# Queries and keys of an attention layer by full Strassen products, in a rewritten fixed order of four engines

## The chip, the cores and the metric

The kernel runs on one core of a Trainium2 chip. The metric is the time of one execution on the device in microseconds (us); the kernel before was run three times, and their median is 1639.4 us. A core has five engines with instruction queues of their own, each worked off in order: PE (matmuls and transposes), DVE and ACT (element-wise work, both also on the accumulators in PSUM), POOL (element-wise work in on-chip memory only) and SP, which here issues the DMAs.

## The reference

A decoder trunk of two layers on one sequence of 1024 tokens with 1024 features, in float32. Layer 0 is attention in three dilated groups, layer 1 a diagonal state-space layer. The change concerns layer 0:

```python
def dilated_attention_mixer(h, w_in, w_out, rel_bias):
    proj = h @ w_in                          # (1024 x 1024) @ (1024 x 10240)
    qkv = proj[..., :n_qkv].reshape(B, S, 3, N_GROUPS_A, ATTN_HEADS, HEAD_DIM)
    z = proj[..., n_qkv:]
    for g, (window, dilation) in enumerate(DILATED_GROUPS):   # (128,1) (512,4) (2048,16)
        o, l = dilated_group_attention(qkv[:, :, 0, g], qkv[:, :, 1, g], qkv[:, :, 2, g], ...)
        ...
    wts = jax.nn.softmax(jnp.stack(lses), axis=0)             # the groups are merged
    o = jnp.sum(wts[..., None] * jnp.stack(outs), axis=0)
    return (o * jax.nn.silu(z)) @ w_out
```

`h` is the normalised input. Before and after the mixer stand an RMS norm each, and the result is added to the input.

## The kernel before

**Precision.** Every operand of a large matmul is split into a high part (rounded to the fast float32 format `F32R`) and a low part (what the rounding left): `split` casts on ACT (L104) and subtracts on another engine (L105). A product then takes three matmuls: high x high, low x high, high x low.

**Strassen.** The normalised rows stand transposed on chip as `c.h[th]`: th is a half of the tokens (512), and each holds eight k-tiles of 128 features, as high and low parts. Taken as 2 x 2 blocks (th, kh), with kh a half of the features, they make a product of 2 x 2 blocks possible with seven block products instead of eight (Winograd's form). The class `Quads` adds up the row sums that this needs, `self.rows = [a11, a12, s4, a22, s1, s2, s3]`; a block has four k-tiles. The values of the attention are made this way early (L440) and go to DRAM (`v_dr`).

**Units.** Queries and keys are made in the attention stage by 24 units, one for a pair of heads p and a group g each. A unit's two raw weight tiles (512 KB each, pool `wraw` with two buffers) are the columns of q and of k: these are the two column halves of the Strassen form. Between the two stages the memory holds only two of four k-tiles of each row sum: the tile of a sum is a `Halves` object of two pieces, one in the pool `pf`, which stays, and one in the pool `vphase`, which is closed. So a unit does seven Strassen products (`form`) on k-tiles 0, 1 of each half, and k-tiles 2, 3 by plain products (`straight`). `product(n)`, n from 0 to 9, accumulates all of this in two PSUM banks, X and Y; `sums(n)` copies or adds what is to be kept, and `qk(n)` splits the results into the tiles q and k that the logits read. All these matmuls have the line L567.

**Order.** The function `attn_units` runs 26 steps. In step m, unit m (`cur`) does its products, unit m-1 (`one`) its logits and exponentials and the first of its weighted sums of values (PV), and unit m-2 (`two`) the rest of them, while the weights of unit m+1 (`nxt`) are loaded and split. The object `Program` pins the order in which the instructions are written for each of PE, ACT, DVE and POOL; SP's order is left to the scheduler. So a helper's instruction that must wait holds up whatever is written behind it on the same engine. On PE the order of a step is

```
product 0, 1 | PV T | logits 0 | product 2, 3 | PV T | logits 1 | product 4, 5 | PV ptm |
logits 2 | product 6, 7 | logits 3 | T | product 8, 9 | PV T
```

where T are the transposes of exponentials (L726), PV is L775, logits are L698 with their bias and maximum on DVE (L704), ptm is the transpose of the statistics in `put_ms` (L802). POOL makes the low parts of the weights (L105) and their differences (L541), the low parts of q and k, the rotations for layer 1 and the merge of the groups (L953, L954). Buffers that the change touches: the bias tile `T` (two), the split exponentials `ph` (three), `vp` for all eight blocks of a unit's values, `wsp` with four weight tiles, and `w5`, `w6` of their own.

**Gates.** After the units, `attn_gate` multiplies both token halves with the columns of z for four pairs of heads (the other four are done early), so it needs all of `c.h` again.

Of the kernel before, what the change touches and what calls it, by code (L numbers as in the profile page):

```python
# [56 lines left out]
class Halves:  # L57


    def __init__(self, *parts):  # L60
        self.parts = parts

    def __getitem__(self, at):
        p, k, cols = at if len(at) == 3 else at + (slice(None),)
        if isinstance(k, slice):
            return self.parts[k.start // 2][p, :, cols]
        return self.parts[k // 2][p, k % 2, cols]
# [181 lines left out]
def load_bias(c, p, g):  # L249


    t = c.attn.tile([P, 2, 256], F32, tag="T", name="T", bufs=2)
    at = 0 if g < 2 else P
    src = bass.AP(c.vec_dr.tensor, c.vec_dr.offset + (g * 16 + 2 * p) * 384 + at, [[1, P], [384, 2], [1, 256 - at]])
    c.nc.sync.dma_start(t[:, :, at:256], src)
    return t


def evac_q(c, ps, g, t0, q):

    n = ps.shape[1] // ORD[g]
    at = (S - t0) // ORD[g] - n
    hi, lo = (t.rearrange("p (r l) -> p r l", r=ORD[g])[:, :, at:at + n] for t in q)
    split(c, hi, lo, ps.rearrange("p (l r) -> p r l", r=ORD[g])[:, :, ::-1], 0.125)

# [43 lines left out]
class Quads:  # L309
# [4 lines left out]
    def __init__(self, c):  # L314
# [3 lines left out]
        def part(th, kh):  # L318
            return [t[:, 4 * kh:4 * kh + 4, :] for t in c.h[th]]
# [3 lines left out]
        def tt(o, x, y, op):  # L323
            for n in (slice(0, 2), slice(2, 4)):
                nc.vector.tensor_tensor(o[:, n], x[:, n], y[:, n], op=op)

        def parts(slots, t):
            hi, lo = (c.vslot(s, F32R) for s in slots)
            for n in (slice(0, 2), slice(2, 4)):
                split(c, hi[:, n], lo[:, n], t[:, n])  # L330
            return hi, lo
# [19 lines left out]
        self.rows = c.forms = [a11, a12, s4, a22, s1, s2, s3]  # L351
        t2, t3 = c.vslot(2, F32), c.vslot(3, F32)
        self.sums = [t2[:, 0:2], t2[:, 2:4], t3[:, 0:2]]
        self.tmp = t3[:, 2:4].rearrange("p a x -> p (a x)")

# [150 lines left out]
class Unit:  # L506
# [6 lines left out]
    def __init__(self, c, m):  # L513
        self.c = c
        self.p, self.g = divmod(m, 3)
        self.engine = c.nc.gpsimd if m else c.nc.vector
        self.p1 = self.u2 = self.u3 = None
        self.lg, self.pt, self.ph, self.po = {}, {}, {}, {}
# [3 lines left out]
    def load(self, w_in):  # L522
        c = self.c
        with c.tc.high_priority(AHEAD):
            self.raw = []
            for n in range(2):
                t = c.wraw.tile([P, KT * P], F32, tag="wraw", name="wraw")
                c.nc.sync.dma_start(t, w_in[(3 * n + self.g) * 8 + self.p])
                self.raw.append(t.rearrange("p (a b x) -> p a b x", a=2, b=2))

    def halves(self, src, tag, pool=None):
        c = self.c
        w = (pool or c.wsp).tile([P, 2] + list(src.shape[1:]), F32R, tag=tag, name=tag, bufs=1 if pool else 4)
        c.last_lo = split(c, w[:, 0], w[:, 1], src, engine=self.engine).ins
        return w

    def weights(self, n):
        c = self.c
        q, k = self.raw
        def sub(o, x, y):  # L540
            self.engine.tensor_tensor(o, x, y, op=ALU.subtract)  # L541

        b11, b21, b12, b22 = q[:, 0, 0], q[:, 1, 0], k[:, 0, 0], k[:, 1, 0]
        if n == 0:
            self.w1 = self.halves(q[:, :, 0], "w")
            sub(b11, b12, b11)
            sub(b12, b22, b12)
        elif n == 1:
            self.w6 = self.halves(b22.unsqueeze(1), "w6", c.attn)
            sub(b22, b22, b11)  # L550
            sub(b21, b21, b22)
        elif n == 2:
            self.w2 = self.halves(q[:, :, 1], "w")
        elif n == 3:
            self.w3 = self.halves(k[:, :, 0], "w")
        elif n == 4:
            self.w4 = self.halves(q[:, :, 0], "w")
        else:
            self.w5 = self.halves(k[:, :, 1], "w5", c.attn)
# [3 lines left out]
    def block(self, ps, w, a, rows, ks, start, stop):  # L563
        c = self.c
        order = [(b, x, y) for b in range(2) for x, y in ((0, 0), (1, 0), (0, 1))]
        for m, (b, x, y) in enumerate(order):
            c.nc.tensor.matmul(ps, w[:, y, a, b * P:b * P + P], rows[x][:, ks + b, :], start=start and m == 0,  # L567
                                      stop=stop and m == 5, skip_group_check=True)

    def form(self, ps, i, w, a, start=False, stop=True):  # L570
        self.block(ps, w, a, self.c.forms[i], 0, start, stop)

    def straight(self, ps, w, th, start=False, stop=True):
        self.block(ps, w, 0, self.c.h[th], 2, start, False)
        self.block(ps, w, 1, self.c.h[th], 6, False, stop)

    def order(self, ps, reverse):

        t = ps.rearrange("p (l r) -> p r l", r=ORD[self.g])
        return t[:, :, ::-1] if reverse else t  # L580

    def copy(self, name):
        t = self.c.slot(name, tag="a").rearrange("p (r l) -> p r l", r=ORD[self.g])
        if name == "p1":
            self.c.nc.scalar.activation(t, self.order(self.X, True), AF.Copy, scale=0.125)
        else:
            self.c.nc.scalar.copy(t, self.order(self.X, False))
        return t

    def add(self, t):  # L590
        v, y = self.c.nc.vector, self.order(self.Y, t is self.p1)
        if t is self.p1:
            v.scalar_tensor_tensor(t, y, 0.125, t, op0=ALU.mult, op1=ALU.add)
        else:
            v.tensor_tensor(t, t, y, op=ALU.add)  # L595

    def bank(self, n):
        c = self.c
        return (c.psx, c.psy)[n].tile([P, H], F32, tag="xy"[n], name="xy"[n])

    def product(self, n):
        if n == 0:
            self.X = self.bank(0)
            self.form(self.X, 0, self.w1, 0, start=True)
        elif n == 1:
            self.Y = self.bank(1)
            self.straight(self.Y, self.w2, 0, start=True, stop=False)
        elif n == 2:
            self.form(self.X, 5, self.w3, 1)
        elif n == 3:  # L610
            self.form(self.Y, 1, self.w1, 1)
        elif n == 4:
            self.form(self.X, 6, self.w3, 0)
        elif n == 5:
            self.Y = self.bank(1)
            self.form(self.Y, 2, self.w6, 0, start=True, stop=False)
            self.straight(self.Y, self.w5, 0)
        elif n == 6:
            self.straight(self.X, self.w2, 1, stop=False)
        elif n == 7:  # L620
            self.Y = self.bank(1)
            self.form(self.Y, 4, self.w4, 0, start=True)
        elif n == 8:
            self.form(self.X, 3, self.w4, 1)
        else:
            self.straight(self.Y, self.w5, 1)

    def sums(self, n):
        if n == 0:
            self.p1 = self.copy("p1")  # L630
        elif n == 2:
            self.u2 = self.copy("u2")
        elif n == 4:
            self.u3 = self.copy("u3")
        else:
            self.add(getattr(self, {3: "p1", 5: "u2", 7: "u2", 9: "u3"}[n]))

    def qk(self, n):
        c, g = self.c, self.g
        if n == 0:  # L640
            self.q, self.k = ([c.attn.tile([P, S], F32R, tag=x + y, name=x + y, bufs=1) for y in "hl"] for x in "qk")
        if n == 1:
            evac_q(c, self.X, g, H, self.q)
            return
        src = (self.p1, None, self.u2, self.u3)[n]
        w = H // ORD[g]
        at = 0 if n == 2 else w
        hi, lo = (t.rearrange("p (r l) -> p r l", r=ORD[g])[:, :, at:at + w] for t in (self.k if n else self.q))
        split(c, hi, lo, src, engine=c.nc.gpsimd)
# [3 lines left out]
    def load_v(self):  # L653
        c, p, g = self.c, self.p, self.g
        self.vp = vp = c.attn.tile([P, KT, P], F32, tag="vp", name="vp", bufs=1)
        o = ORD[g]
        off = c.v_dr.offset + (g * 2 + p // 4) * S * H + p % 4 * P
        for dst, at, step in (((vp, 0, P),), ((vp[:, 0::2], 0, 1), (vp[:, 1::2], o * P, 1)), ((vp, 0, 1),))[g]:
            src = bass.AP(c.v_dr.tensor, off + at * H, [[o * H, P], [step * H, dst.shape[1]], [1, P]])
            c.nc.sync.dma_start(dst, src)  # L660
        self.bt = load_bias(c, p, g)

    def split_v(self):
        c, vp = self.c, self.vp
        self.v = vs = c.attn.tile([P, KT, 2, P], F32R, tag="vs", name="vs", bufs=1)
# [63 lines left out]
    def split_weights(self, u, x):  # L729
        c = self.c  # L730
        parts = []
        for pt, wd in self.pt.pop((u, x)):
            t = c.attn.tile([P, 2, H], F32R, tag="ph", name="ph", bufs=3)
# [148 lines left out]
def attn_units(c, w_in):  # L882
# [7 lines left out]
    for n in (0, 2, 1, 3, 4, 5):  # L890
        units[0].weights(n)
    for m in range(26):
# [13 lines left out]
        if m:  # L906
            run((cur, "weights", 5))
        if one and one.g == 0:
            step(rotations, c, one.p, 0)
            step(rotations, c, one.p, 1)  # L910
        if two and c.merge is not None:
            if two.g == 0:
                step(merge_weights, c, c.merge)
            step(merge, c, c.merge, c.outputs[c.merge], two.g)
# [1089 lines left out]
```

## Time and profile before

| | |
|---|---|
| three runs | 1637.63, 1639.40, 1639.65 us |
| profiled execution | 1634.66 us, its span 1632.8 us |
| granted TensorE clock | 0.996 |
| busy share PE / DVE / ACT / POOL | 98 / 65 / 47 / 42% |
| attention stage (first to last matmul of L567) | about 339 to 1062 us |

The lines of the profile name line, engine and operation, what is written and what is read, the shapes, the count, then the busy time of the group in us, the mean of one instruction in ns, and the idle time of the engine before them with what ended it. Timeline rows give start and duration in us. Rows of stretches give, for each engine, busy us and number of instructions, then the TensorE clock, the DMA engines' share and GB/s. The matmul durations overlap, as matmuls are pipelined; their starts tell the pace.

### The profile page before, as it was taken

What the parts mean: (1) busy time and instruction counts of PE and PEld (TensorE: products, weight loads), DVE (VectorE), ACT (ScalarE), POOL (GpSimd) and SP (SyncE); (2) the same over time, 40 slices, a digit from 0 to 9 for tenths busy, and PEclk for the clock granted to TensorE, in tenths of its full rate; (3) what the DMA queues carried; (4) which work ended last, traced back from release to release, by engine and by line L of the source; (5) the groups of instructions that cost most, each with busy time, mean ns of one, the idle gap of its engine ahead of it and who ended that gap; (6) DMA issues with size and microseconds to landing.
All of it is one profiled execution on the core that took longest, in us unless ns stands there. A gap on an engine that the chain in (4) does not pass through costs nothing.

```text
span 1632.8 us, 26979 instructions
## 1 busy us (share of the span) xinstructions
PE 1606.7 (98%) x9606; PEld 1368.8 (84%) x9606; DVE 1060.0 (65%) x2563; ACT 773.9 (47%) x1904; POOL 689.7 (42%) x579
## 2 busy tenths in 40 slices
PE   8999999999999999999999999999999999989998
PEld 6889999988888888888888888887888888878886
DVE  8799899835565565655565565748563899855533
ACT  5232233236656666666666666655353233334411
POOL 1000000055557767675768767533220455422121
PEclk9999999999999999999999999999999999999999
DMA  6123445442232332333233332327346988665532
GB/s 253 65 53 110 157 146 162 138 148 58 77 95 82 98 111 72 101 95 96 80 92 111 86 124 79 122 66 196 128 152 184 262 247 241 198 194 161 174 101 86
DMA packets 184720, 212.24 MB, mean 130 GB/s; under 512 B 42484, under 2 KB 138503, under 8 KB 184585
## 3 DMA queue, kind: packets, MB, share of 16 engines
q1 hardware_dynamic: 184584, 210.52, 43.0%
q8 instruction: 75, 1.23, 0.3%
q14 instruction: 61, 0.49, 0.1%
HBM read 153.51 MB, written 56.96 MB: 129 GB/s over the span
## 4 chain that ended last, share of the span: by engine, by line
PE 88%; DVE 6%; DMA 4%; issue 1%; POOL 1%; ACT 1%; SPq 0%; DVEq 0%; ACTq 0%; POOLq 0%
PE y L567 18%; PE psj L130 16%; PE x L567 13%; PE psq L440 10%; PE pso L1180 10%; PE pso L775 5%; PE psl L698 5%; PE pt L726 4%; PE psv L298 2%; PE psb L130 1%; DMA v<-in_x_dram 1%; DVE T L1706 1%; PE pst L147 1%; DVE T L1711 1%; PE pv L1699 1%
## 5 line engine op out<-in xcount | busy, mean ns | idle before, releaser
L567 PE MATMUL y<-hh,w 128*128 128x512 f32 x672 | 225.5, 393 | 0.0
L105 POOL TENSOR_TENSOR w<-wraw,w 128x512 fp32r<-128x512 f32 x138 | 164.5, 1199 | 135.0 <-ACT w L104 130.3
L720 ACT ACTIVATE lg<-lg,nm 128x128 f32<-128x128 f32 (+1 forms) x384 | 168.5, 442 | 36.7 <-DVE nm L715 36.5
L567 PEld LDWEIGHTS y<-hh,w 128*128 128x128 f32 x672 | 126.3, 188 | 28.9
L567 PE MATMUL x<-hh,w 128*128 128x512 f32 x384 | 138.0, 410 | 0.0
L567 PE MATMUL y<-hl,w 128*128 128x512 f32 x336 | 131.6, 392 | 0.0
L1558 POOL TENSOR_TENSOR Ks<-Ks,O 128x16 f32<-128x16 f32 x8 | 3.8, 476 | 292.6 <-ACT Ks L1556 292.6
L595 DVE TENSOR_TENSOR u<-u,y 128x512 f32<-128x512 f32 x72 | 49.4, 687 | 118.4 <-PE y L567 118.4
L704 DVE CUSTOM_DVE_ANT_0 lg<-psl,T 128x128 f32<-128x128 f32 (+1 forms) x384 | 110.6, 347 | 12.8 <-PE psl L698 10.3
L440 PE MATMUL psq<-whi,v 128*128 128x256 f32 x640 | 118.4, 282 | 0.0
L775 PEld LDWEIGHTS pso<-ph,vs 128*128 128x128 f32 x736 | 100.4, 189 | 11.5 <-ACT ph L104 1.9
L105 DVE TENSOR_TENSOR ph<-pt,ph 128x512 fp32r<-128x512 f32 (+2 forms) x160 | 93.9, 620 | 19.1 <-ACT ph L104 17.6
L130 PE MATMUL psj<-h1h,whi 128*128 128x512 f32 (+1 forms) x272 | 103.0, 384 | 1.1 <-ACT h1h L104 1.1
L795 DVE TENSOR_TENSOR O<-O,pso 64x512 f32<-64x512 f32 x64 | 44.2, 691 | 89.6 <-ACT O L794 89.6
L775 PE MATMUL pso<-ph,vs 128*128 128x256 f32 (+1 forms) x736 | 100.1, 276 | 2.1 <-ACT ph L104 1.5
L130 PE MATMUL psj<-h1l,whi 128*128 128x512 f32 (+1 forms) x272 | 101.8, 379 | 0.2 <-DVE h1l L105 0.2
L440 PEld LDWEIGHTS psq<-whi,v 128*128 128x128 f32 x640 | 99.3, 188 | 1.8 <-issue 1.2
L104 ACT CAST w<-wraw 128x512 fp32r<-128x512 f32 x144 | 81.5, 578 | 25.6 <-POOL wraw L541 19.0
L104 ACT CAST ph<-pt 128x512 fp32r<-128x512 f32 (+2 forms) x160 | 78.4, 531 | 30.4 <-PE pt L726 28.6
L1207 POOL TENSOR_TENSOR xr<-xr,y 128x512 f32<-128x512 f32 x30 | 38.2, 1295 | 126.3 <-DVE y L1206 99.1
L440 PE MATMUL psq<-wlo,v 128*128 128x256 f32 x320 | 89.6, 281 | 0.9 <-DVE wlo L105 0.9
L104 ACT CAST whi<-v 128x1024 fp32r<-128x1024 f32 x35 | 36.7, 1050 | 112.9 <-PE psq L440 87.0
(302 smaller groups left out, 4538.7 us busy)
## 6 DMA issues: line engine op xcount, KB each, us to landing
wraw<-in_w_in_dram SPq DMA_DIRECT2D x56, 512.0 KB
v<-in_w_v_dram SPq DMA_DIRECT2D x24, 512.0 KB
mw<-wt_dr SPq DMA_DIRECT2D x84, 128.0 KB
vp<-v_dr SPq DMA_DIRECT2D x16, 512.0 KB
wraw<-in_ssm_w_in_dram SPq DMA_DIRECT2D x16, 512.0 KB
v_dr<-v SPq DMA_DIRECT2D x30, 256.0 KB
ca_dr<-ca SPq DMA_DIRECT2D x32, 144.0 KB
CA<-ca_dr SPq DMA_DIRECT2D x8, 576.0 KB
```

What stands on the lines that cost most here:

```text
L104: c.last_hi = nc.scalar.copy(hi, src).ins
L105: return (engine or nc.vector).tensor_tensor(lo, src, f32(hi), op=ALU.subtract)
L130: nc.tensor.matmul(ps, w[n == 2][:, k * P:k * P + P], h[n == 1][:, k, :], start=first and k == 0 and m == 0, stop=m == len(order) - 1 and ...
L440: nc.tensor.matmul(o, r[x][:, k, ts], w[y][:, k, :], skip_group_check=True, start=i in (0, 4, 5) and t % 2 == k == n == 0, stop=k == 3 and ...
L567: c.nc.tensor.matmul(ps, w[:, y, a, b * P:b * P + P], rows[x][:, ks + b, :], start=start and m == 0, stop=stop and m == 5, skip_group_chec ...
L595: v.tensor_tensor(t, t, y, op=ALU.add)
L698: nc.tensor.matmul(psl[:, h, o], x[HEADS[h], qs], y[HEADS[h], ks], start=j == js[0] and i == 0, stop=i == 2, skip_group_check=True)
L704: nc.vector.tensor_tensor_reduce(self.lg[u, j][:, h], psl[:, h, o], self.bt[:, h, 256 - w:256], scale=1.0, scalar=-3.0e38, op0=ALU.add, op ...
L720: c.nc.scalar.activation(t, t, AF.Exp, bias=self.nm[:, h, b:b + 1], accum_out=ms[:, col:col + 1])
L726: c.nc.tensor.transpose(pt[:, n * P:(n + 1) * P], self.lg[u, j][:, h, part * P:part * P + P], c.ident)
L775: nc.tensor.matmul(o, l, r, start=n == 0, stop=n == len(jobs) - 1, skip_group_check=True)
L1180: nc.tensor.matmul(ps, x[:, k, ts], y[:, k, cols], start=n == m == 0, stop=n == KT - 1 and m == len(todo) - 1)
```

## The change

All four k-tiles of each half go through the Strassen products: a unit has seven products of four k-tiles, with 12 matmuls each, and no plain ones. For this the row sums stay whole in `pf`. Block a21 (second token half, first feature half; high and low part) isn't one of the seven rows; it now lives in `vphase`, is written to a DRAM tensor `a21_dr` when the row sums are made, and is read back into a new pool `pa3` when `attn_gate` begins. The products are numbered like the values' (0, 1, 5, 6, 4, 3, 2, in this order), each with one weight tile `w` of [128, 2, 512]. The differences of weights are made over 512 columns, partly on DVE. The last low part of k moves from POOL to DVE (`evac_k`). The values are loaded and split in two halves, the bias tile has one buffer and `ph` two. The merge and the rotations become generators whose operations are spread over the step by `more(n)`; the negation of a rotation goes from POOL to ACT. The load of the next unit's weights moves from the start of the step to behind the last weight split. Cut to what matters:

```diff
 class Quads:
         def part(th, kh):
-            return [t[:, 4 * kh:4 * kh + 4, :] for t in c.h[th]]
+            return [t.parts[kh] for t in c.h[th]]
         def tt(o, x, y, op):
-            for n in (slice(0, 2), slice(2, 4)):
-                nc.vector.tensor_tensor(o[:, n], x[:, n], y[:, n], op=op)
+            nc.vector.tensor_tensor(o, x, y, op=op)
...
+        for n in range(2):
+            nc.sync.dma_start(c.a21_dr[n].rearrange("p (k x) -> p k x", k=4), f32(a21[n]))
 class Unit:
+    def difference(self):
+        self.c.nc.vector.tensor_tensor(self.b12, self.b22, self.b12, op=ALU.subtract)
+
+    def weights(self, i):
+        one, two = c.nc.vector, c.nc.vector if self.first else c.nc.gpsimd
+        if i == 5:
+            one.tensor_tensor(b11, b12, b11, op=ALU.add)
+        src = {0: b11, 1: b21, 5: b11, 6: b12, 4: b11, 3: b21, 2: b22}[i]
+        w = self.w[i] = c.wsp.tile([P, 2, H], F32R, tag="w", name="wqk")
+        c.last_lo = split(c, w[:, 0], w[:, 1], src, engine=two).ins
+        if i == 5:
+            two.tensor_tensor(b21, b21, b11, op=ALU.subtract)
+            two.tensor_tensor(b11, b22, b11, op=ALU.subtract)
     def product(self, i):
+        ps = self.X if i in (0, 5, 6, 3) else self.Y
+        w, rows = self.w.pop(i), c.forms[i]
+        order = [(b, x, y) for b in range(4) for x, y in ((0, 0), (1, 0), (0, 1))]
+        for m, (b, x, y) in enumerate(order):
+            c.nc.tensor.matmul(ps, w[:, y, b * P:b * P + P], rows[x][:, b, :], start=i in (0, 1, 4) and m == 0,
+                               stop=m == len(order) - 1, skip_group_check=True)
     def sums(self, i):
+        # 0: p1 = X (ACT)   1: p1 += Y (DVE)   5: u2 = X (ACT)   6: u3 = X (ACT)
+        # 4: u3 += Y (DVE)  2: Y += u2 (DVE, in PSUM)
     def qk(self, i):
+        # 3: q from X   2: k from Y (ACT and DVE)   1: q from p1   4: k from u3 (ACT and POOL)
 def attn_units(c, w_in):
-        if nxt:
-            nxt.load(w_in)
-        run((cur, "product", 0), (two, "split_weights", 0, 1), (cur, "sums", 0))
...
+        run((cur, "product", 0), (cur, "sums", 0), (two, "PV", 0, 1), (two, "T", 1, 0),
+            (two, "split_weights", 1, 0), (two, "exps", 1, 1), (two, "store", 0, 1), (cur, "weights", 6), (cur, "weights", 4))
+        if weigh is not None:
+            step(merge_weights, c, weigh)
+        else:
+            more(1)
+        run((cur, "product", 1), (cur, "sums", 1), (one, "logits", 0),
+            (two, "PV", 1, 0), (two, "T", 1, 1), (two, "split_weights", 1, 1), (two, "store", 1, 0), (cur, "weights", 3))
+        more(2)
+        run((cur, "product", 5), (cur, "sums", 5), (one, "logits", 1), (two, "PV", 1, 1))
         if two:
             c.pair = two.p
             step(put_ms, c, two.g, two.ms)
+        run((one, "split_v", 0), (one, "load_v", 1), (two, "store", 1, 1), (one, "exps", 0, 0), (cur, "weights", 2),
+            (nxt, "load", w_in))
+        more(5)
+        run((cur, "product", 6), (cur, "sums", 6), (one, "logits", 2), (one, "exps", 0, 1), (cur, "product", 4),
+            (cur, "sums", 4), (one, "T", 0, 0), (one, "split_weights", 0, 0), (one, "split_v", 1), (cur, "load_v", 0),
+            (one, "logits", 3), (nxt, "difference"), (nxt, "weights", 0), (cur, "qk", 1), (cur, "qk", 4), (cur, "product", 3), (cur, "qk", 3),
+            (nxt, "weights", 1), (one, "PV", 0, 0), (one, "T", 0, 1), (one, "split_weights", 0, 1),
+            (one, "store", 0, 0), (one, "exps", 1, 0), (cur, "product", 2), (cur, "sums", 2), (cur, "qk", 2), (nxt, "weights", 5))
+        more(9)
 def attn_gate(c, a, h):
+    a21 = [row_tile(c.pa3, 1, 0, x) for x in "hl"]
+    for n in range(2):
+        nc.sync.dma_start(f32(a21[n]), c.a21_dr[n].rearrange("p (k x) -> p k x", k=4))
+    h = [h[0], [Halves(t, x.parts[1]) for t, x in zip(a21, h[1])]]
```

The two comments in `sums` and `qk` stand for their code; removed lines are shown only where they are moved.

More of the change, by code (lines that the diff above doesn't have):

```diff
@@ L264, in evac_q, with evac_k @@
     split(c, hi, lo, ps.rearrange("p (l r) -> p r l", r=ORD[g])[:, :, ::-1], 0.125)
+def evac_k(c, ps, g, t0, k):
+    n = ps.shape[1] // ORD[g]
+    at = t0 // ORD[g]
+    hi, lo = (t.rearrange("p (r l) -> p r l", r=ORD[g])[:, :, at:at + n] for t in k)
+    split(c, hi, lo, ps.rearrange("p (l r) -> p r l", r=ORD[g]))
 def first_values(c, a, rows):
@@ L563, in block @@
[L563 to L571, printed above, removed]
@@ L590, in add @@
[L590 to L626, printed above, removed]
@@ L628, in sums @@
[L628 to L649, printed above, removed]
@@ L889, in attn_units @@
     units[0].load(w_in)
-    for n in (0, 2, 1, 3, 4, 5):
-        units[0].weights(n)
+    for i in (0, 1, 5):
+        if i == 5:
+            units[0].difference()
+        units[0].weights(i)
     for m in range(26):
@@ L945, in merge @@
     nc = c.nc
+    halves = [slice(n * H, n * H + H) for n in range(2)]
     for g in ((2, 0), (1,))[part]:
-        for n in range(2):
-            cols = slice(n * H, n * H + H)
+        for n, cols in enumerate(halves):
             w = c.slot("mw", tag="b")
@@ L953, in merge @@
             nc.gpsimd.tensor_tensor(O[g][:, cols], O[g][:, cols], w, op=ALU.mult)
-    nc.gpsimd.tensor_tensor(O[2], O[2], O[part], op=ALU.add)
+            yield
+    for cols in halves:
+        nc.gpsimd.tensor_tensor(O[2][:, cols], O[2][:, cols], O[part][:, cols], op=ALU.add)
+        yield
     if part == 0:
@@ L957, in merge @@
     if p >= EARLY:
-        for n in range(2):
-            cols = slice(n * H, n * H + H)
+        for cols in halves:
             w = c.slot("mg", tag="b")
@@ L1612, in store @@
             nc.sync.dma_start(dst, t[HEADS[s]].rearrange("p (k x) -> p k x", k=4))
-    with c.tc.issue_after(c.last_lo):
+    for part in range(2):
         out, tmp = c.slot("rt", tag="b"), c.slot("rtmp", tag="b")
```

215 lines of the change are left out of this document (104 added, 111 removed).

## The prediction

> **What bounds the kernel now.** I read the page's head, then the engines' busy time in six equal stretches of the attention stage, then the page's chain.
>
> ```profile
> span 1632.8 us, 26979 instructions
> PE 1606.7 (98%) x9606; PEld 1368.8 (84%) x9606; DVE 1060.0 (65%) x2563; ACT 773.9 (47%) x1904; POOL 689.7 (42%) x579
> 440.00:532.70 92.70, 92.70 (x580) 77.98 (x579) 53.61 (x161) 60.19 (x175) 64.64 (x55) 1.00 0.31 92
> 903.50:996.20 92.70, 92.70 (x582) 78.06 (x581) 53.40 (x163) 60.32 (x175) 67.12 (x56) 1.00 0.33 99
> PE y L567 18%; PE psj L130 16%; PE x L567 13%; PE psq L440 10%; PE pso L1180 10%; PE pso L775 5%; PE psl L698 5%; PE pt L726 4%; PE psv L298 2%; PE psb L130 1%; DMA v<-in_x_dram 1%; DVE T L1706 1%; PE pst L147 1%; DVE T L1711 1%; PE pv L1699 1%
> ```
>
> Columns of the stretches: PE, PEld, DVE, ACT, POOL, TensorE clock, DMA share, GB/s. The stage repeats every 92.7 us for three units (30.9 us each), PE without a gap at clock 1.00, DVE, ACT and POOL at 58, 65 and 70% of it. The chain runs through L567, the products that the change touches, with 31% of the span. A busy PE could hide slack, so the starts of matmuls decide:
>
> ```profile
> 642.58 1.55 PE L567 MATMUL y<-v,w 128*128 128x512 f32 x6
> ...
> 646.71 0.88 PE L775 MATMUL pso<-ph,vs 128*128 128x256 f32 x6
> 647.43 0.27 PE L802 MATMUL ptm<-identr,ms 128*32 128x128 f32 x1
> 647.63 0.39 PE L698 MATMUL psl<-kl,qh 64*128 64x256 f32 x2
> ...
> 648.33 0.28 PE L698 MATMUL psl<-kh,qh 64*128 64x256 f32 x2
> 648.54 0.50 PE L567 MATMUL x<-hh,w 128*128 128x512 f32 x1
> 648.87 0.39 PE L567 MATMUL x<-hl,w 128*128 128x512 f32 x1
> 649.11 0.62 PE L567 MATMUL x<-hh,w 128*128 128x512 f32 x2
> ```
>
> From 642.58 to 646.71 stand the 18 matmuls of one accumulation: 4.13/18 = 0.23 us each, back to back. The first product after logits starts 0.2 us late in all: 0.21 after the last pair, where pairs follow each other by 0.11 (below), and 0.33 to its successor instead of 0.23.
>
> **The products.** Before, seven products each cover four of eight k-tiles (two a half) with 6 matmuls, 42, and the other four k-tiles are done straight, four blocks of 12, 48: 90 a unit. After, seven products of 4 k-tiles by 3 matmuls: 84. The rows count the 90 (24 units, 2160):
>
> ```profile
> L567 PE MATMUL y<-hh,w 128*128 128x512 f32 x672 | 225.5, 393 | 0.0
> L567 PE MATMUL x<-hh,w 128*128 128x512 f32 x384 | 138.0, 410 | 0.0
> L567 PE MATMUL y<-hl,w 128*128 128x512 f32 x336 | 131.6, 392 | 0.0
> L567 PE MATMUL x<-v,w 128*128 128x512 f32 x288 | 79.5, 410 | 0.2 <-DVE w L105 0.2
> L567 PE MATMUL x<-hl,w 128*128 128x512 f32 x192 | 75.6, 394 | 0.0
> L567 PE MATMUL y<-v,w 128*128 128x512 f32 x288 | 74.5, 394 | 0.0
> ```
>
> 24 x 6 = 144 matmuls go, at 0.23 us: **-33.1 us**. The mean of 0.39 us in these rows contains pipelining and would overstate it. The Trainium skill (TensorE: Matmul & The Clock Gate, Back-to-back issue gap) gives about 131 ns for such a matmul in a sustained stream with weight loads, by which the sum would lose only 144 x 0.131 = 18.9 us (an estimate from that page). The starts here contradict it, so the 0.23 stands.
>
> **Changes of kind on PE.** New neighbours are logits before PV (twice a unit) and logits 3 before a product instead of before transposes.
>
> ```profile
> 653.43 0.28 PE L698 MATMUL psl<-kh,ql 64*128 64x128 f32 x2
> 653.54 0.28 PE L698 MATMUL psl<-kh,qh 64*128 64x128 f32 x2
> 653.75 1.09 PE L726 MATMUL pt<-identr,lg 128*128 128x128 f32 x8
> ```
>
> Logits to transposes cost 0.1 (0.21 against 0.11), logits to a product 0.2. Before: three of the dear kind and one cheap, 0.7. No row has logits before PV; at 0.1 to 0.2 each a unit costs 0.6 to 0.8, so -2.4 to +2.4 us in all. PV reads split halves as products do, so I take 0.2: **+2.4**.
>
> **The other engines, per unit.** Rows of the stage from 440 to 1040 us:
>
> ```profile
> L105 POOL TENSOR_TENSOR w<-wraw,w 128x512 fp32r<-128x512 f32 x98 | 125.8, 1292 | 84.5 <-ACT w L104 80.8 <-DMA rot_dr<-rtmp 3.8
> L541 POOL TENSOR_TENSOR wraw<-wraw 128x256 f32<-128x256 f32 x76 | 72.4, 953 | 6.0
> L953 POOL TENSOR_TENSOR O<-O,mw 128x512 f32<-128x512 f32 x36 | 46.1, 1297 | 47.3 <-DMA mw<-wt_dr 47.1
> L105 POOL TENSOR_TENSOR w<-wraw,w 128x256 fp32r<-128x256 f32 x19 | 14.0, 736 | 4.6 <-ACT w L104 4.6
> L104 ACT CAST w<-wraw 128x512 fp32r<-128x512 f32 x97 | 58.2, 612 | 17.3 <-POOL wraw L541 17.3
> L720 ACT ACTIVATE lg<-lg,nm 128x256 f32<-128x256 f32 x146 | 73.0, 502 | 15.9 <-DVE nm L715 15.7
> L595 DVE TENSOR_TENSOR u<-u,y 128x512 f32<-128x512 f32 x58 | 39.8, 686 | 92.1 <-PE y L567 92.1
> L794 ACT COPY O<-pso 64x512 f32<-64x512 f32 x50 | 28.9, 578 | 19.7 <-PE pso L775 19.1
> L104 ACT CAST vs<-vp 128x1024 fp32r<-128x1024 f32 x19 | 19.8, 1043 | 0.0
> L815 ACT COPY mt<-ptm 32x128 f32<-32x128 f32 x12 | 3.1, 254 | 26.5 <-PE ptm L802 26.5
> L587 ACT COPY u<-x 128x512 f32<-128x512 f32 x38 | 22.4, 589 | 57.9 <-PE x L567 57.8
> ```
>
> POOL now makes five low parts of 1.29, one of 0.74, four differences of 0.95, three low parts of q and k (1.3): 14.9. After: seven, two differences of 512 columns (1.3 by the nearest row), two low parts: 14.3. The merges' full-width adds become halves, and the negation of a rotation goes to ACT. ACT gains a cast of 0.6 and half of another, 0.9. DVE gains two differences and k's low part, loses one add: 2 x 0.69. So DVE and ACT come to some 65 and 72% of a shorter unit; none becomes the bound by volume. Off PE's path: 0.
>
> What can cost is order, as each engine runs its list in the written order. I walked the new list with these durations.
>
> *Next unit's weights.* `nxt.load` moves from the unit's first step to behind `weights(2)`, past vp, bias and statistics DMAs in SP's queue. Raw weights have two buffers, so the k load waits for POOL's low part. From `put_ms` on, ACT does its copy, half of vs, a store, four exponentials and the cast: 0.25 + 0.55 + 0.58 + 2.0 + 0.6 = 4.0; POOL's part ends at 5.3. A DMA to its use takes about 3.4 us by these rows (two dependent ones, issue to the merge's multiply, 6.7):
>
> ```profile
> 760.29 0.62 SPq L849 DMA_DIRECT2D wt_dr<-cm  x1
> 767.02 1.30 POOL L953 TENSOR_TENSOR O<-O,mw 128x512 f32<-128x512 f32 x1 [7.47 <-DMA mw<-wt_dr]
> ```
>
> That gives 8.7 for q, and 10.8 for k if its 0.52 MB go behind q's at 249 GB/s (row below). POOL meanwhile does up to five merge operations (6.5) and is free at 11.8; the low part of `weights(0)` ends at 13.1. PE needs it after four products (2.76 each), two logits (0.9 each, 647.63 to 648.54), two groups of transposes (0.7 each for six, by the row of eight) and one PV (0.7): 14.9. Slack about 2 us. `nxt.difference` waits for k on DVE until 10.8; behind it stands only the split of q's second half, whose bank X is next written at 14.9.
>
> *Banks.* Products 5 and 6 both accumulate in X with u2's copy (0.59) between; logits 1, PV and put_ms (1.8 us of PE) cover it. Without cover, in the first unit, it costs about 1 us: **+1**. Product 2's bank Y is added, cast and subtracted (0.69 + 0.6 + 0.69) before the next product 1, covered by product 0, PV and transposes (4.2). DVE must finish logits 0 before logits 1 overwrites the bank; between lie PV, transposes and product 5. Two ph buffers instead of three make a split wait for the last PV; each has a product before its own PV. One bias tile makes its load wait for logits 3, half a unit before its use. The second half of vp has product 6, logits 2, product 4 and T (7 us) against 3.4. All: 0, as long as a product stays between.
>
> **Kept off chip.** 2.1 MB are written after the rows and read back for the gates.
>
> ```profile
> 80.00:120.00 40.00, 39.54 (x189) 32.49 (x188) 37.19 (x77) 14.32 (x18) 0.00 (x0) 1.00 0.24 51
> 1280.00:1320.00 40.00, 40.00 (x230) 34.84 (x229) 36.88 (x48) 10.51 (x18) 21.25 (x19) 1.00 0.83 249
> 70.22 44.58 PE psj L130 x191
> ```
>
> At 249 GB/s each way is 8.4 us. The write lies under 44.58 us of gate matmuls with DMA at 0.24: 0. The read needs memory that product 6 of the last unit frees, some 15 us ahead of the first gate, which itself takes 24 x 0.23 = 5.5 before this quarter is wanted. At worst (issued only when the last product ends, 3.4 + 8.4 - 5.5) 6 us; I take **+1**. The undivided sums of the forms save DVE instructions under the same gates: 0.
>
> **Sum.** -33.1 + 2.4 + 1 + 1 = -29 us. The profiled execution is 1634.7 (its span and 1.9), 4.7 below the median of 1639.4; from it 1606, from the median 1610. I say 1609.
>
> **Rivals.**
> *Some waits appear.* A slack of 2 us is thin: the mw wait of 7.47 sits on POOL ahead of `weights(2)` in every third unit. For it: SP is in order and its raw loads already wait for POOL. Against: ACT's and POOL's idle time above. At 0.6 us a unit, 24 x 0.6 gives back 14: 1624. One more reason is in the durations of L541, 0.73 to 1.61 us for one shape. The Trainium skill (SBUF — State Buffer, Who interferes with whom) says a DVE operation with two SBUF inputs locks out a GpSimd read for its whole length; DVE gets two such per unit, an estimated 1.4 us of POOL's slack by the row of 0.69.
>
> *The gain is cancelled.* Were a product's wait 1.2 us in each unit, 24 x 1.2 = 29: 1638, no change.
>
> *Slower: the raw load comes too late.* If SP puts the bias load, which waits for logits 3 (about 9 us after put_ms), ahead of both raw loads, and they take 6.7 as the pair above, `weights(0)` is cast at 16.3 and ready at 17.6, against 14.9: 2.7 us each unit, 65 - 29, 1675. It decides from 1.2 us of lateness on, a landing after 14.2. Against it: the order of issue is free, and the bias load is written later.
>
> **How the numbers follow.** Saturated PE 0.62 (1603 to 1616, by the boundary, read-back and first-unit bounds); some waits 0.21 (1616 to 1635); cancelled 0.06; slower 0.11. Two executions of this kernel differ by 0.1%, so 0.2%, 3.3 us, is what can be told. Faster 0.83, same 0.06, slower 0.11. The range 1602 to 1636 leaves out the slower rival, half of the cancelled one and a tail below.
>
> **What would show it.** 2016 matmuls on the products' line in place of 2160, still 0.23 apart; three units in about 89 us with PE full; no idle PE before a product that names the low part of w. Wrong would be: PE gaps released by w, x or y in every unit, a DMA of raw weights as what ACT or DVE waits for, or a long PE gap before the second gate half.

## The result: 1648.9 us, slower by half a per cent, and the profile after

The changed kernel takes 1648.9 us (median of ten runs, 1642.4 to 1656.9) beside 1639.5 us for the kernel before in the same runs; the ratio is 1.0056, 95% interval 1.0034 to 1.0078. The forecast was 1609 us, in a range that ended at 1636. The profiled execution took 1648.7 us, its span 1646.9 us.

The head of the page after, which answers to the first two lines shown of before:

```profile
span 1646.9 us, 26841 instructions
PE 1594.8 (97%) x9462; PEld 1354.6 (82%) x9462; DVE 1119.7 (68%) x2620; ACT 794.3 (48%) x1956; POOL 680.3 (41%) x538
```

PE has 144 matmuls fewer (9462 for 9606), as the change says, and is busy 11.9 us less; the span is 14.1 us longer. So PE now waits. I cut the attention stage at the statistics transposes (`ptm`), of which each step has one. Three steps of before, then three of after, in stretches with the columns of the prediction (PE, PEld, DVE, ACT, POOL, TensorE clock, DMA share, GB/s):

```profile
432.70:462.10 29.40, 29.40 (x181) 24.57 (x181) 15.32 (x49) 18.52 (x55) 22.31 (x21) 1.00 0.36 94
462.10:494.50 32.40, 32.40 (x207) 27.35 (x206) 21.07 (x61) 21.51 (x60) 18.34 (x16) 1.00 0.32 101
494.50:525.50 31.00, 31.00 (x200) 26.16 (x198) 17.32 (x53) 20.17 (x59) 24.09 (x20) 1.00 0.25 82
```

```profile
427.80:456.00 28.20, 28.20 (x177) 23.33 (x176) 16.78 (x60) 18.69 (x57) 17.28 (x15) 1.00 0.24 72
456.00:491.30 35.30, 32.16 (x201) 26.95 (x199) 25.31 (x68) 23.00 (x63) 18.91 (x15) 0.97 0.32 84
491.30:521.50 30.20, 30.20 (x193) 25.30 (x192) 17.86 (x48) 21.35 (x61) 23.41 (x18) 0.98 0.34 102
```

The plain step fell from 29.4 to 28.2, and 1.2 us is most of the 1.4 that six matmuls at 0.23 us give: the saving is there. The step at 456 rose from 32.4 to 35.3, with PE idle 3.14 us and the clock at 0.97, and the step behind it lost part of its gain, at 0.98. There are seven such steps: those in which unit `two` is the first of its pair of heads (from the second pair on), so that the merge of the pair before has its maxima and weights made. I call them merge steps. What PE waited for from 440 to 1040 us (us in all, number of waits, the longest), and one place:

```profile
PE psl L665 <- DVE ms L671: 19.5, 6, 3.8
```

```profile
676.85 0.58 PE L665 MATMUL psl<-kl,qh 64*128 64x256 f32 x2 [3.14 <-DVE ms L671]
...
678.32 1.97 PE L742 MATMUL pso<-ph,vs 128*128 128x256 f32 x8
680.09 0.41 PE L769 MATMUL ptm<-identr,ms 128*32 128x128 f32 x1
680.15 4.61 PE L570 MATMUL x<-v,wqk 128*128 128x512 f32 x12
684.70 0.39 PE L665 MATMUL psl<-kl,qh 64*128 64x256 f32 x2
```

Logits 1 waits for DVE's reduces (L671) of logits 0, which holds the only buffer of the pool `psa`. A seventh wait of this kind lies behind 1040 us; the seven take 23.0 us. And behind the wait everything is slow: product 6 takes 4.55 us from its first start to the next work, where twelve matmuls at 0.23 are 2.8. The clock around this place:

```profile
670.70:673.70 3.00, 3.00 (x14) 2.13 (x12) 2.93 (x3) 2.06 (x5) 3.00 (x3) 1.00 0.00 0
673.70:676.80 3.10, 0.01 (x1) 0.00 (x0) 3.00 (x13) 0.58 (x1) 0.55 (x1) 1.00 0.05 8
676.80:683.60 6.80, 6.75 (x29) 5.96 (x30) 4.51 (x14) 1.95 (x6) 0.65 (x1) 0.50 0.57 157
683.60:690.00 6.40, 6.40 (x47) 5.00 (x46) 1.99 (x10) 4.74 (x19) 5.73 (x6) 1.00 0.76 225
```

The granted clock is 0.50 for 6.8 us from the end of the gap on. The same goes with each of the seven gaps (3.14 us five times, 3.77, 3.55), for 6.8 or 3.4 us, from between 1.1 us before the gap's end and 0.5 behind it. The kernel before had no such stretch in this stage.

Why are the reduces late? DVE's timeline, and POOL's beside it:

```profile
670.48 1.39 DVE L810 TENSOR_TENSOR cm<-cm,cm 64x96 f32<-64x96 f32 x1
671.90 1.17 DVE L811 TENSOR_TENSOR cm<-cm 64x32 f32<-64x32 f32 x1
673.10 1.20 DVE L812 TENSOR_TENSOR cm<-cm,cm 64x32 f32<-64x32 f32 x1
674.34 0.35 DVE L813 RECIPROCAL cm<-cm 64x32 f32<-64x32 f32 x1
674.72 0.25 DVE L814 SCALAR_TENSOR_TENSOR cm<-cm,cm 64x96 f32<-64x96 f32 x1
675.00 0.69 DVE L580 SCALAR_TENSOR_TENSOR p<-y,p 128x512 f32<-128x512 f32 x1
675.61 0.41 DVE L671 CUSTOM_DVE_ANT_0 lg<-psl,T 128x256 f32<-128x256 f32 x1
```

```profile
670.47 1.29 POOL L105 TENSOR_TENSOR wqk<-wraw,wqk 128x512 fp32r<-128x512 f32 x1 [2.30 <-ACT wqk L104]
671.71 1.30 POOL L105 TENSOR_TENSOR wqk<-wraw,wqk 128x512 fp32r<-128x512 f32 x1
672.99 1.27 POOL L105 TENSOR_TENSOR wqk<-wraw,wqk 128x512 fp32r<-128x512 f32 x1
```

L810 to L814 are `merge_weights`, which the new order puts ahead of `sums(1)` and logits 0. They are tiny (64 x 96 or 64 x 32), yet the first three end at 671.87, 673.07 and 674.30, each 0.04 to 0.11 us after one of POOL's low parts ends (671.76, 673.01, 674.26). They get in one at a time, when a POOL instruction is over. Once POOL is done, the last two take 0.35 and 0.25. In the kernel before, only the third of them was held up:

```profile
L845 DVE TENSOR_TENSOR cm<-cm,cm 64x32 f32<-64x32 f32 x7 | 8.1, 1157 | 0.2
...
L843 DVE TENSOR_TENSOR cm<-cm,cm 64x96 f32<-64x96 f32 x7 | 1.7, 241 | 0.0
L844 DVE TENSOR_TENSOR cm<-cm 64x32 f32<-64x32 f32 x7 | 1.3, 184 | 0.2
```

Theory A, then: `merge_weights`, stretched by POOL from 1.2 to 4.5 us, stands in front of what frees the logits bank; PE waits 3.1 us, and the gap halves the clock. Rivals: B, the denser products bring the clock down by themselves; C, the five operations are slow by themselves; D, the wait costs and the lower clock is hidden.

### The profile page after: what moved, and what is told of

It reads as the page before. It is cut to its first block, busy times and chain, and to the rows that moved or that the text cites. A ratio compares the mean times of both kernels' runs of the same rounds, so it can differ in the third digit from the quotient of the medians.

```text
span 1646.9 us, 26841 instructions
## 1 busy us (share of the span) xinstructions
PE 1594.8 (97%) x9462; PEld 1354.6 (82%) x9462; DVE 1119.7 (68%) x2620; ACT 794.3 (48%) x1956; POOL 680.3 (41%) x538
## 4 chain that ended last, share of the span: by engine, by line
PE 65%; DVE 10%; ACT 4%; issue 2%; DMA 2%; POOL 1%; SPq 0%; DVEq 0%; ACTq 0%; POOLq 0%
PE x L570 14%; PE psj L130 11%; PE pso L1160 10%; PE y L570 10%; PE psq L449 5%; PE pso L742 5%; PE psl L665 4%; PE pt L693 3%; ACT lg L687 2%; PE psb L130 1%; DVE T L1684 1%; DVE T L1689 1%; ACT ph L104 1%; DVE ph L105 1%; DVE O L762 1%
## 5 line engine op out<-in xcount | busy, mean ns | idle before, releaser
L105 POOL TENSOR_TENSOR wqk<-wraw,wqk 128x512 fp32r<-128x512 f32 x161 | 212.9, 1330 | 118.7 <-ACT wqk L104 116.9
L570 PE MATMUL x<-v,wqk 128*128 128x512 f32 x576 | 153.8, 417 | 0.7 <-ACT u L583 0.7
L570 PE MATMUL y<-v,wqk 128*128 128x512 f32 x576 | 145.4, 401 | 0.0
L671 DVE CUSTOM_DVE_ANT_0 lg<-psl,T 128x128 f32<-128x128 f32 (+1 forms) x384 | 110.5, 346 | 38.9 <-PE psl L665 38.5
L570 PE MATMUL x<-hh,wqk 128*128 128x512 f32 x384 | 130.8, 401 | 0.0
L570 PEld LDWEIGHTS x<-v,wqk 128*128 128x128 f32 x576 | 110.3, 199 | 24.4 <-ACT u L583 1.1
L570 PEld LDWEIGHTS y<-v,wqk 128*128 128x128 f32 x576 | 105.3, 188 | 23.9
L104 ACT CAST wqk<-wraw 128x512 fp32r<-128x512 f32 x168 | 102.1, 618 | 40.0 <-DVE wraw L550 31.6
L742 PE MATMUL pso<-ph,vs 128*128 128x256 f32 (+1 forms) x736 | 109.1, 291 | 2.1 <-ACT ph L104 1.4
L570 PEld LDWEIGHTS x<-hh,wqk 128*128 128x128 f32 x384 | 72.2, 188 | 17.7
```

Of the source, the lines that this page charges most:

```text
L104: c.last_hi = nc.scalar.copy(hi, src).ins
L105: return (engine or nc.vector).tensor_tensor(lo, src, f32(hi), op=ALU.subtract)
L570: c.nc.tensor.matmul(ps, w[:, y, b * P:b * P + P], rows[x][:, b, :], start=i in (0, 1, 4) and m == 0, stop=m == len(order) - 1, skip_group ...
L671: nc.vector.tensor_tensor_reduce(self.lg[u, j][:, h], psl[:, h, o], self.bt[:, h, 256 - w:256], scale=1.0, scalar=-3.0e38, op0=ALU.add, op ...
L742: nc.tensor.matmul(o, l, r, start=n == 0, stop=n == len(jobs) - 1, skip_group_check=True)
```

## The experiments

Ratios are to the kernel before, run beside each on the same chip, with 95% intervals.

**Behind logits 0 (e1).** Ratio 1.0063 (1.0042 to 1.0083).

```diff
-        if weigh is not None:
-            step(merge_weights, c, weigh)
-        ...
         run((cur, "product", 1), (cur, "sums", 1), (one, "logits", 0),
-            (two, "PV", 1, 0), ...
+        )
+        if weigh is not None:
+            step(merge_weights, c, weigh)
+        ...
+        run((two, "PV", 1, 0), ...
```

> The merge weights' five small VectorE operations stand behind logits 0's reduces in place of ahead of them. Theory A (these operations, stretched to 4.5 us by GpSimd's low parts beside them, hold the one logits bank, and TensorE's wait for it halves the clock): in the seven merge steps the 3.14-us wait ahead of logits 1 goes, and with it the stretches of clock 0.5; the operations now delay the last split and PV(1,1) by about 1.5 us. 1649 - 7 x (3.1 + 1.7 - 1.5) = 1626 us; 1605 if PV does not wait. Rival B (the clock falls for the denser products themselves, and the wait is not what costs): within 0.3% of 1649. Rival C (the operations are slow by themselves and GpSimd has no part in it) expects the same as A here.

Measured 1653.1 us beside 1642.2, 27 us over the forecast. What PE waited for from 440 to 1040 us, and POOL:

```profile
PE x L570 <- POOL wqk L105: 12.3, 6, 3.5
PE pso L742 <- DVE ph L105: 8.0, 6, 1.7
```

```profile
POOL O L929 <- DMA mw<-wt_dr: 64.2, 18, 8.3
```

The wait ahead of logits 1 is gone and PV waits 1.3 us in the mean, as expected. What I had left out: the merge weights go to DRAM and come back as `mw` for POOL's multiplications. Now they leave later, POOL stands 64.2 us for them (38.9 in the changed kernel), and the low part of the next unit's `weights(0)` is queued behind. PE then waits for it, up to 3.5 us, in the step after.

**POOL quiet (e2).** Ratio 0.9887 (0.9870 to 0.9903).

```diff
-            (two, "store", 0, 1), (cur, "weights", 6), (cur, "weights", 4))
+            (two, "store", 0, 1))                # in merge steps, weights 6 and 4
...
+        if weigh is not None:                    # come behind store(1, 0)
+            run((cur, "weights", 6), (cur, "weights", 4))
```

> The merge weights stay where the change put them; in the merge steps alone the low parts of products 6 and 4 are made one job later, so that GpSimd is idle while the five small operations run. Theory A: the operations take 1.2 us in sum in place of 4.5, the wait ahead of logits 1 is under 0.5 us, the clock stays at 1.00: between 1605 and 1616 us. Rival C (they are slow by themselves, or for their own chain of results): the operations stay at 4.5 us, the wait at 3.1, the time at 1649. Rival B (clock): operations faster, time within 0.3% of 1649.

Measured 1623.1 us. `merge_weights` stands where the change put it, with the same operands; only POOL is idle beside it. Groups of DVE from 440 to 1040 us:

```profile
L810 DVE TENSOR_TENSOR cm<-cm,cm 64x96 f32<-64x96 f32 x7 | 1.8, 250 | 0.1
...
L812 DVE TENSOR_TENSOR cm<-cm,cm 64x32 f32<-64x32 f32 x7 | 1.3, 183 | 0.2
L811 DVE TENSOR_TENSOR cm<-cm 64x32 f32<-64x32 f32 x7 | 1.3, 182 | 0.2
```

With the two left out (0.35 and 0.25) they are 1.2 us instead of 4.4, and the wait ahead of logits 1 fell from 3.1 us to 0.7 at most. C falls. So does B: the products are as dense, and in the stage the clock does not fall before 1046 us, behind the last product. The time is 7 us above the expected range's end.

**PE kept busy through the wait (e3).** Ratio 1.0033 (1.0020 to 1.0046).

```diff
+        if weigh is not None:
+            step(two.warm)      # 12 matmuls into the bank of PV(1, 1), overwritten by it
         run((one, "logits", 1), (two, "PV", 1, 1))
```

> Twelve matmuls whose result nobody reads (some 2.8 us) stand behind product 5 in the merge steps, into the bank that PV(1,1) takes next, so that TensorE is busy while it would wait for logits 1's bank. Theory A: the wait is as long (its part without work under 0.5 us), but the granted clock stays at 1.00 and product 6 takes 2.8 us in place of 3.9 to 4.3: 1649 - 7 x 2 = 1635 us. Rival B (the clock falls for dense products): it falls here too, and more work stands before it: 1649 or more. Rival D (the wait alone costs, the lower clock is hidden): 1649.

Measured 1647.6 us. The place of 676 us in its timeline, and its merge step with the one behind:

```profile
671.02 2.93 PE L730 MATMUL pso<-hh 128*128 128x512 f32 x12
674.68 0.39 PE L665 MATMUL psl<-kl,qh 64*128 64x256 f32 x2 [0.74 <-DVE ms L671]
```

```profile
641.80:676.50 34.70, 33.96 (x213) 28.28 (x211) 25.07 (x62) 23.00 (x63) 19.87 (x16) 1.00 0.33 83
676.50:707.70 31.20, 30.16 (x192) 24.77 (x191) 18.59 (x54) 21.46 (x61) 22.85 (x18) 1.00 0.38 106
```

The clock stays at 1.00 through the seven merge steps, though logits 1 waits no less: the gap is what halves it, not the products. But the gain is 0.0023 of the time, 4 us, with intervals that overlap, not 14. The same steps of the changed kernel are 35.8 and 31.2 us long. The merge step gained 1.1 us; in the next, PE idles 1.04 us at full clock, for DVE's low part of q among others. The comparison isn't pure: from logits 0 to logits 1 it is 9.1 us here (665.60 to 674.68) and 8.7 in the changed kernel (668.14 to 676.85), so some 2.6 us of the clock's worth may be lost again in seven steps. Even so D is nearer to the size than A: most of the lower clock was hidden, and the wait itself is the larger part.

**One place earlier (e4, timed again as e11).** Ratios 0.9854 (0.9839 to 0.9869) and 0.9865 (0.9842 to 0.9888).

```diff
-            step(merge_maxima, c)         # from the head of the merge step
-            step(merge_weights, c, weigh)
...
-        run((cur, "product", 0), (cur, "sums", 0), (two, "PV", 0, 1), ...
+        run((cur, "product", 0), (cur, "sums", 0))
+        if weigh is not None:
+            step(merge_weights, c, weigh)
+        run((two, "PV", 0, 1), ...
...
+                step(merge_maxima, c)     # at the end of the step before
```

> The merge maxima stand at the end of the step before and the merge weights right behind sums 0, one job ahead of where the change has them. GpSimd's sums and low parts run beside them there, so by theory A they are stretched too (3 to 5 us), but VectorE then has the time for it: the wait ahead of logits 1 goes; PV(1,0) may wait about 1 us for its split. 1649 - 7 x (4.8 to 6.5) + 7 x 1 = 1610 to 1622 us. Rival B: within 0.3% of 1649. Rival C: as A.

> The version with the merge maxima at the end of the step before and the merge weights right behind sums 0, timed once more in more rounds beside the kernel before: ratio 0.985, 1617 to 1619 us; by the rival that its first timing was luck against the version in VectorE's gap, 0.988.

Measured 1617.8 and 1618.4 us, beside 1642.2 and 1638.6. PE's wait ahead of logits 1 is gone; PV waits 0.4 to 1.1 us instead.

**In DVE's gap (e5), and the maxima earlier too (e7).** Ratios 0.9878 (0.9861 to 0.9896) and 0.9877 (0.9862 to 0.9891).

```diff
         run(..., (two, "T", 1, 0), (two, "split_weights", 1, 0))
+        if weigh is not None:
+            step(merge_weights, c, weigh)
+        run((two, "exps", 1, 1), (two, "store", 0, 1), ...
```

> One job earlier than in the changed kernel, behind the split of weights (1,0) and ahead of store(0,1): there VectorE stands idle 1.69 us for ScalarE's copy, and GpSimd is idle from 668.2 to 670.5 us of the changed kernel's trace. Theory A: the five small operations take 1.2 us in that gap and cost nothing, no wait of TensorE over 0.4 us in the merge steps, merge steps 31.1 to 31.5 us long: 1613 to 1618 us, at or below the version with the weights behind sums 0 (1617.8), where PV(1,0) waited up to 1.1 us. Rival (the gap is gone once TensorE no longer stalls, and the operations delay store(0,1) or logits 0's reduces): wait of 0.5 to 1.2 us, 1619 to 1625 us.

> As the version with the merge weights in VectorE's gap, and the merge maxima at the end of the step before, so that ScalarE's exponential of them stands ahead of sums 0's copy in time. Theory: 0 to 5 us below that version (0.7 us of ScalarE ahead of the split's cast in each of seven merge steps, hidden or not): 1612 to 1617 us. Rival: VectorE waits there for the DMA that loads the maxima and is late for the next step's first work: 1618 to 1625 us.

Measured 1620.1 and 1619.0 us. Three steps of e5, which answer to the first three of before:

```profile
427.50:455.60 28.10, 28.10 (x175) 23.24 (x174) 16.71 (x59) 18.69 (x57) 17.17 (x15) 1.00 0.24 73
455.60:486.80 31.20, 31.20 (x203) 26.11 (x200) 22.02 (x68) 23.00 (x63) 19.57 (x16) 1.00 0.39 104
486.80:516.30 29.50, 29.50 (x191) 24.82 (x191) 17.56 (x50) 21.23 (x61) 22.98 (x18) 1.00 0.32 94
```

28.1, 31.2 and 29.5 for 29.4, 32.4 and 31.0: 88.8 us for 92.8, PE without a gap. This is the forecast's "three units in about 89 us". But not every triple is so short. Steps of the third kind take up to 32.0 us (664.9 to 696.9), and there one finds:

```profile
679.67 1.84 DVE L542 TENSOR_TENSOR wraw<-wraw 128x512 f32<-128x512 f32 x1 [2.49 <-DMA wraw<-in_w_in_dram]
681.43 0.68 DVE L108 SCALAR_TENSOR_TENSOR ql<-x,qh 128x512 fp32r<-128x512 f32 x1
```

`nxt.difference` waits for raw weights, takes 1.84 us beside a busy POOL, and q's low part, which frees bank X, stands behind it; PE waits 1.55 us. With the stalls gone, this rival of the prediction is next: DVE waited 9.4 us for raw weights in five steps (1.6 in the changed kernel). The gap and the place behind `sums(0)` cannot be told apart by their intervals.

**A sum with one operand (e6).** Ratio 0.9957 (0.9940 to 0.9973).

```diff
-    nc.vector.tensor_tensor(den, s[:, 0], s[:, 1], op=ALU.add)
-    nc.vector.tensor_tensor(den, den, s[:, 2], op=ALU.add)
+    nc.vector.reduce_sum(den, s.rearrange("p g n -> p n g"), axis=mybir.AxisListType.X)
```

> Order as in the changed kernel, GpSimd as busy; but the two additions of the denominators (each with two operands in SBUF) are one reduction over the three groups with one operand in SBUF. Theory L (VectorE waits for the end of GpSimd's running instruction only where its own instruction reads two operands in SBUF): the reduction takes 0.2 to 0.4 us beside GpSimd, the product ahead of it 1.39 and the last multiplication up to 1.2; the wait ahead of logits 1 falls from 3.1 to 0.8 to 1.5 us and the time to between 1620 and 1638 us. Rival M (every small VectorE instruction waits while GpSimd works): the reduction takes 1.2 us too and the wait 2.5 to 3.1 us: 1640 to 1650 us.

Measured 1631.5 us. DVE and POOL of one merge step:

```profile
665.26 1.38 DVE L810 TENSOR_TENSOR cm<-cm,cm 64x96 f32<-64x96 f32 x1
666.68 0.25 DVE L811 TENSOR_REDUCE cm<-cm 64x32 f32<-64x96 f32 x1
666.97 0.35 DVE L812 RECIPROCAL cm<-cm 64x32 f32<-64x32 f32 x1
667.35 0.57 DVE L813 SCALAR_TENSOR_TENSOR cm<-cm,cm 64x96 f32<-64x96 f32 x1
```

```profile
665.25 3.81 POOL L105 TENSOR_TENSOR wqk<-wraw,wqk 128x512 fp32r<-128x512 f32 x3 [2.31 <-ACT wqk L104]
```

The reduction, with one operand in SBUF, takes 0.25 us while POOL runs; the product ahead of it, with two, still 1.38, and the last multiplication, also with two, 0.57 where it took 0.25. The instructions that wait for POOL here are those with two SBUF operands, not all of DVE's. PE's wait fell to 1.3 to 1.95 us.

**The raw load on POOL's queue (e8, e9), and POOL's merge behind it (e10).** Ratios 1.0147 (1.0127 to 1.0167), 1.0221 (1.0202 to 1.0240) and 1.0208 (1.0193 to 1.0224).

```diff
-                c.nc.sync.dma_start(t, w_in[(3 * n + self.g) * 8 + self.p])
+                (c.nc.sync if self.first or n == 0 else c.nc.gpsimd).dma_start(t, w_in[...])
```

e8 is e5 and e9 is e4, each with this line changed; e10 is e8 with POOL's merge operations (`more(5)`) of the merge steps put behind `(nxt, "weights", 1)`.

> As the version with the merge weights in VectorE's gap; but the second of the next unit's two loads of raw weights (512 KB) is issued by GpSimd, right behind the low part that frees its tile, in place of by SyncE's queue, where it stands behind five loads of merge weights in the step after each merge (issued at 674.86 us of that version's trace, after them from 670.95). In that version VectorE waited 9.4 us in five steps for this load ahead of the difference, and the products waited behind it up to 1.55 us. Theory R (the load's place in SyncE's queue is what is late): VectorE's waits for it go, steps of the first kind at 29.5 us, 4 to 6 us less than that version: 1614 to 1616 us. Rival S (the load is bound by the transfer, or GpSimd issues more slowly than SyncE): waits as long or longer, 1620 to 1630 us.

> The same load issued by GpSimd, in the version with the merge weights right behind sums 0 (1617.8 us, with 3.7 us of VectorE's waits for the load). Theory R: 2 to 3 us less, 1615 us. Rival S: 1618 to 1628 us.

> As the version with the second raw load on GpSimd (1666.8 us), but in the merge steps GpSimd's multiplications and additions of the merged outputs stand behind the low part of the next unit's weights 1, in place of ahead of its low parts of weights 0, queries and keys. In that version VectorE's low part of the values (vp, vs: two operands in SBUF) began at 682.83 us and ended at 691.95, while GpSimd ran eight instructions without a pause from 681.52 to 691.48. Theory A carried over (VectorE's instruction with two SBUF operands gets in only where GpSimd stops): GpSimd now pauses there, waiting for ScalarE's cast, VectorE's low part takes 0.7 to 2 us, TensorE's waits of 5.2 to 6.2 us in seven steps go: 1612 to 1625 us. Rival T (the load issued by GpSimd is itself what is slow): the waits stay, 1660 us or more.

Measured 1666.8, 1679.0 and 1673.0 us, all three far above what was expected. In e8 DVE waited 1.8 us in two steps for raw weights, for 9.4 in five. That speaks for the load's place as what was late, but doesn't show it, as seven of e8's steps are some 8 us longer and give the load time. POOL, which paused 1.07 us for an `mw` load between two multiplications in e5's step, here has them in time and runs on, and DVE's low part of the values, with two SBUF operands, does not get in for a long time:

```profile
682.83 9.20 DVE L105 TENSOR_TENSOR vs<-vp,vs 128x512 fp32r<-128x512 f32 x1
```

```profile
681.52 2.56 POOL L930 TENSOR_TENSOR O<-O,mw 128x512 f32<-128x512 f32 x2
684.03 2.53 POOL L933 TENSOR_TENSOR O<-O,O 128x512 f32<-128x512 f32 x2
...
690.23 1.25 POOL L105 TENSOR_TENSOR wqk<-wraw,wqk 128x512 fp32r<-128x512 f32 x1
```

It starts as the second of POOL's eight instructions does and ends 0.5 us after the last; PE waited 5.2 to 6.2 us in seven steps (4.6 to 5.7 in eight in e9). In e10 POOL pauses there, and the low part takes 0.68 us in the step that I read; in two later steps POOL runs seven instructions without a pause again, the low part takes 8.5 us, and PE waits 4.9 and 5.5 us. In the other steps ACT's store of the next output now waits up to 7.4 us for POOL's last addition, which frees the buffer, and PE waits 2.9 to 3.6 us ahead of transposes. None of these gave a faster kernel; e4 has the lowest ratio of all that ran.

## Why the prediction was wrong

*The products, -33.1 us: right.* L570 has 2016 matmuls for 2160, and a step without other trouble lost 1.2 to 1.5 us, 4.0 in three (e5); eight times that is 32, beside the 33.1 of this term and the 30.7 of this one and the next together.

*Changes of kind, +2.4: not contradicted.* Logits before PV, in e5, and PV behind a product:

```profile
663.94 1.16 PE L742 MATMUL pso<-ph,vs 128*128 128x256 f32 x8
...
676.11 1.02 PE L742 MATMUL pso<-ph,vs 128*128 128x256 f32 x8
```

PV starts 0.22 us after the last pair of logits (663.72), where pairs follow each other by 0.11, and eight of its matmuls then take 1.16 us for 1.02. That is some 0.2 in all, the dear value that was taken.

*Banks, "All: 0, as long as a product stays between": the step that failed.* The walk took from PV to product 5 as cover for DVE's reduces, and left out that in every third step DVE has `merge_weights` to do first. It is in the diff, ahead of `product(1)` and logits 0. Even walked, it would have been costed at 2.2 us by the rows of before, as one of five was stretched there. The measured cost is 4.5 us of DVE, 3.14 us and more of PE, 23.0 us over seven steps, and a clock of 0.5 with each gap. From the first product to the output projection, after takes 801.5 us and e5 769.9: of these 31.6 us, 23.0 are the waits. The other 8.6 are not separated; the lower clock is in them.

*Contention of DVE and POOL.* I had used the rule of the Trainium skill (SBUF — State Buffer, Who interferes with whom) only against POOL's slack. That section says that whichever of the two issues first keeps the shared ports for its whole instruction while the other is blocked, and that a reduction never contends on trn2. The rows agree on both: 1.17 to 1.39 us for operations of 0.18 to 0.25, and 0.25 for the reduction. It bites in the direction that I did not cost.

*Next unit's weights, slack about 2 us, 0: nearly.* 1.6 us of DVE's waits in the changed kernel; 9.4 in e5, where PE lost 2.0 to it directly. The slack is nearer 0 than 2 once the stalls no longer cover it.

*First unit, +1, and the read-back, +1.* PE waits 0.68 us for u2's copy in the first unit. The block kept off chip is read back from 1077.8 us on, behind the last product, and no wait of PE from there to the output projection at 1137.0 ends on a DMA: the read-back costs PE nothing. The first product starts at 335.5 us for 333.6 before; whether writing the block has a part in that was not tried.

*The sum, without the failed step.* By the two timings of e4 the change would be worth 24 and 20 us, not 29. In e5 some 5 us are in five steps of the third kind (30.1, 32.0, 29.9, 30.9 and 29.9 for 29.5). From the first to the last matmul of the products' line it is 727.7 us before, 705.3 in e5 and 707.4 in e4, so 20 to 22 us of the expected 30.7 are there. Outside of that stretch these two take more than before: they start it some 1.5 us later and need 513.9 and 515.1 us from the output projection to the end, for 509.8 (509.9 in the changed kernel), and e5 takes 64.7 us from the last product to the projection, for 61.7. These are single executions, and that of before was 4.7 us below its median; what makes the difference stays open.

## What to carry to other kernels

Before moving a small operation ahead of one that frees the only buffer of a PSUM pool, list everything that its engine does between the two matmul groups, in every kind of step. Price a VectorE instruction with two SBUF operands at the GpSimd instruction that may run beside it, not at its own length, or give it one operand (a reduction), or a place where GpSimd is idle. When an engine gains slack, look at what its new pace shuts out.

## What the hardware showed

A gap of PE need not be long to halve its clock. With 3.14 us it fell each time; after 1.33 us too, in e1:

```profile
864.81 1.22 PE L742 MATMUL pso<-ph,vs 128*128 128x256 f32 x7 [1.33 <-DVE ph L105]
```

```profile
865.50:868.90 3.40, 3.40 (x12) 2.82 (x11) 3.13 (x12) 1.51 (x4) 0.00 (x0) 0.50 0.69 218
```

But four of e6's seven gaps, of 1.3 to 1.7 us, left it at 1.00, and so did one of 2.05 us in e7. The Trainium skill (TensorE: Matmul & The Clock Gate, What's actually happening) tells of a free-running window of about 3.4 us after which an idle array gets half the clock. The lengths, 3.4 and 6.8 us, agree; that a gap far shorter than the window can be enough is not what "idle window" suggests, and which gaps are enough is left open.

Between back-to-back POOL instructions DVE's small operations got in one by one in the changed kernel, but in e8 a 128 x 512 one did not while seven of them ran. What decides this was not tried.
